# A decoder trunk on one core: the second layer's Gram masks, a pair's norm and T's diagonal blocks, each issued at another place

## The chip, the cores and the metric

The kernel runs on one core of a Trainium2 chip. Five engines take instructions from queues of their own, in order: TensorE (PE, matmuls and transposes; its weight loads are listed apart as PEld), VectorE (DVE), ScalarE (ACT), GpSimd (POOL) and SyncE (SP, which here only issues DMAs). An instruction starts when its engine is free and the semaphores it waits for are set. Matmul results land in PSUM, everything else is kept in SBUF. The metric is the time of the whole program on the device in microseconds (us); a change of 0.2% is 4.4 us here.

## What is computed

Two residual layers over 512 tokens of width 2048. Layer 0 is gated differential attention, layer 1 gated RWKV-7 time mixing. The change touches layer 1 alone. Cut to that layer:

```python
hn = rms_norm(x, norm_w[1])
p = hn @ w_in;  p = p + (token_shift(p) - p) * mu        # r, k, v, g, and two low-rank inputs
r, k, v, g, dw, da = split(p)
decay = exp(-exp(w_log(dw)));  a = sigmoid(a0 + da @ iclr_up)
kk = normalise(k * k_k);  k = k * (1 + (a - 1) * k_a)    # kk: per head of 64 channels
for t in range(512):                                     # per head, state S is 64 x 64
    S = S * decay_t + (S @ -kk_t) outer (kk_t * a_t) + v_t outer k_t
    y_t = S @ r_t
y = (y - mean) * rsqrt(var + eps) * gn_w + gn_b          # over a head's 64 channels
y = y + sum(r * k * r_k) * v
x = x + (y * silu(g)) @ w_out
```

All matrices are float32; products of large matrices are made from split operands (high and low part), three matmuls for each.

## The kernel before

**Pairs and periods.** Layer 1 handles the 32 heads as 16 pairs of heads (128 channels each), in `layer1`. For pair j it computes four projections, each of 16 row blocks times 3 matmuls of 128x512 (48 matmuls `pp` at L129): key (`proj(1, j)`), receptance (`proj(0, j)`, in `receptances`), value (`proj(2, j)`) and gate (`proj(3, ...)`, which lags three pairs behind). These matmuls fill PE; everything else of PE is put between them at counted places. One turn of the loop over j, from one value projection to the next, is called a period here.

**The scan.** The 512 steps of a head are cut into 8 chunks of 64 (C=64), and each chunk is handled by three dependent matmuls, all into one PSUM tile `sm`: a *state product* `sm<-VS,G` (L1341), copied out by ACT as `rhs` (L1344); a *solve product* `sm<-rhs,TT` (L1354), copied by ACT into `VS` (L1356); and an *update* `sm<-VS,BKT` (L1361), from which DVE makes the next chunk's state in `VS` (L1365, with `Sg` from POOL). The chunks are called steps 0 to 7. POOL saves each step's state first (`SA<-VS`, L1349, one copy for each head), and ACT may only overwrite `VS` with the solve product once POOL has done that. After step 7 the outputs `Y` are formed on PE from `VS` and `SA` (L1383, L1387) and centred by DVE (`centre`). Pair j-1's scan runs during pair j's period.

**The Gram matrices.** In pair j's value projection, behind its sixth row block, `gram` multiplies keys by queries: 16 matmuls into four PSUM tiles `gp`. ACT copies them to `G` in SBUF (L1140) and then copies the 32x32 diagonal blocks from `G` to `LP` (L1145). POOL zeroes the halves of `G` that lie beyond the diagonal with four `affine_select` (`mask_gram`, L1171 and L1173). For all pairs but the last that call hangs on the receptance projection of the next pair, but nothing ties the instructions to that matmul: the scheduler, which orders each engine's queue by dependencies and priority, puts them right behind the copies of `G`. The pair's scan reads `G` from the next period on.

**The triangular solve.** `t_solve` inverts the 32x32 blocks of all chunks at once on DVE: a transpose `LT<-LP` (L1202), then 31 steps of two small instructions (`tmpl` L1215, `Tm` L1218), two transposes to `T1` and `W`, and four POOL copies `TT<-W` (L1234). Its steps are let go by the count of projection matmuls that have been issued (`yield`), the first after 12. `t_first` and `t_second` complete `TT` on PE and ACT.

**A pair's norm.** `group_norm` takes ACT's square (`ysq`, L1408), DVE's sum, an inverse root of 11 small DVE instructions (`rs_i`, `rs_t`, L63 to L70) and the scaling of `yc` (L1414).

**Weights.** Each quarter of a 2048-row block of weights is split by ACT (`wh`, L115) and DVE (`wl`, L116) into tiles that are reused as PE finishes with them; these two instructions stand at many places between the others on both engines.

**Order.** Priorities (`high_priority` with AHEAD 2000, SOLVE 4000, SCAN 5000) and `issue_after` decide where the scheduler places an instruction. `behind` adds a dependency without a semaphore: it orders the schedule, but the engine does not wait for it.

Of the kernel before, what the change touches and what calls it, by code (L numbers as in the profile page):

```python
# [13 lines left out]
F32 = mybir.dt.float32  # L14
# [4 lines left out]
ALU = mybir.AluOpType  # L19
# [4 lines left out]
P = 128  # L24
# [14 lines left out]
AHEAD, SCAN, SOLVE = 2000, 5000, 4000  # L39
# [1086 lines left out]
def gram(g, j, p):  # L1126

    nc, w, BK = g.nc, g.work, p.BK
    p.G = w.tile([P, NC_, 2, 2, C], F32, name="G1", tag="G1", bufs=2)
    halves = []  # L1130
    for c0, tag in ((0, "pb"), (4, "pc")):
        gp = [g.ps.tile([P, 512], F32, name="gp", tag=tag, bufs=2) for _ in range(2)]
        halves.append((c0, gp))
        for i in range(4):
            for h, r_ in ((0, slice(0, C)), (1, slice(C, P))):
                m = nc.tensor.matmul(gp[h][:, i * P : (i + 1) * P], BK[r_, c0 + i, :, :], p.AR[r_, c0 + i, :, :],
                                     start=True, stop=True)
    for c0, gp in halves:
        for h in range(2):
            nc.scalar.copy(p.G[:, c0 : c0 + 4, :, h, :], gp[h][:].rearrange("p (u x t) -> p u x t", u=4, x=2))  # L1140
    p.LP = w.tile([P, NC_, HALF], F32, name="LP", tag="tmpl", bufs=1)
    for h in range(2):
        for half in range(2):
            q = slice(h * C + half * HALF, h * C + half * HALF + HALF)
            nc.scalar.copy(p.LP[q], p.G[q, :, 0, h, half * HALF : (half + 1) * HALF])  # L1145


def norms(g, j, p, m):
# [15 lines left out]
    nc.gpsimd.dma_start(out=p.n2[:], in_=nd.rearrange("h b r c t -> (h b r c) t"))  # L1164


def mask_gram(g, p, h):

    nc = g.nc
    for r_ in [slice(h * C, h * C + C)]:  # L1170
        nc.gpsimd.affine_select(out=p.G[r_, :, 0, 1 - h, :], in_=p.G[r_, :, 0, 1 - h, :], compare_op=ALU.is_ge,  # L1171
                                fill=0.0, base=-1, pattern=[[0, NC_], [1, C]], channel_multiplier=-1)
        nc.gpsimd.affine_select(out=p.G[r_, :, 1], in_=p.G[r_, :, 1], compare_op=ALU.is_ge, fill=0.0, base=0,  # L1173
                                pattern=[[0, NC_], [0, 2], [1, C]], channel_multiplier=-1)


def turn_keys(g, p, c0):
# [7 lines left out]
    nc.scalar.copy(p.BKT[:, c0 : c0 + 4], ps[:].rearrange("p (c k) -> p c k", c=4))  # L1185


def behind(g, ins):

    if g.at:  # L1190
        g.tc.add_manual_dep(ins.ins, g.at.ins.name, mybir.DependencyInfo(mybir.DependencyClass.NoSync,
                            mybir.DependencyReason.DATA), reason="pace")


def t_solve(g, j, p):


    nc, w = g.nc, g.work
    NQ = HALF // NG
    yield 12  # L1200
    LT = w.tile([P, HALF, HALF], F32, name="LT", tag="LT", bufs=1)
    lt = nc.vector.transpose(LT[:].rearrange("p (r c) t -> p t r c", r=NG),  # L1202
                        p.LP[:].rearrange("p c t -> p t c")[:, :, None, :].to_broadcast([P, HALF, NG, NC_]))
    Tm = w.tile([P, NQ, HALF], F32, name="Tm", tag="Tm", bufs=1)
    tmp = w.tile([P, NQ * HALF], F32, name="tmpl", tag="tmpl", bufs=1)
    nc.gpsimd.tensor_copy(Tm[:], g.unit[:])
    n2 = p.n2
    behind(g, lt)
    with g.tc.issue_after(lt.ins):
        nc.vector.tensor_scalar(n2[:], n2[:], 1e-24, None, ALU.max)  # L1210
        nc.vector.reciprocal(n2[:], n2[:])
    for i in range(HALF - 1):
        n, s = HALF - 1 - i, i // NG + 1
        tt = tmp[:, : n * s].rearrange("p (a b) -> p a b", a=s)
        st = nc.vector.scalar_tensor_tensor(tt, LT[:, i : i + 1, i + 1 :].to_broadcast([P, s, n]), n2[:, i : i + 1],  # L1215
                                       Tm[:, 0:s, i : i + 1].to_broadcast([P, s, n]), ALU.mult, ALU.mult)
        behind(g, st)
        nc.vector.tensor_add(Tm[:, 0:s, i + 1 :], Tm[:, 0:s, i + 1 :], tt)  # L1218
        yield 3 + i % 2
    nc.vector.tensor_mul(Tm[:], Tm[:], n2[:, None, :].to_broadcast([P, NQ, HALF]))  # L1220
    p.T1 = w.tile([P, NC_, HALF], F32, name="T1", tag="T1", bufs=1)
    yield 9
    tt = nc.vector.transpose(p.T1[:].rearrange("p c (q r) -> p q r c", r=NG),
                        Tm[:].rearrange("p q (r c) -> p q r c", r=NG))
    p.W = w.tile([P, NC_, HALF], F32, name="W", tag="Tm", bufs=1)
    behind(g, tt)
    yield 4
    tt = nc.vector.transpose(p.W[:], p.T1[:])
    behind(g, tt)
    for h in range(2):  # L1230
        for half in range(2):
            o = half * HALF
            q = slice(h * C + o, h * C + o + HALF)
            nc.gpsimd.tensor_copy(g.TT[j % 2][q, :, h, o : o + HALF], p.W[q])  # L1234
# [168 lines left out]
def group_norm(g, j, p):  # L1403
    p.chain.finish(g)
    nc, w, yc = g.nc, g.work, p.yc
    NG = 2 * NT
    sq = w.tile([P, NG, C], F32, name="ysq", tag="thg", bufs=1)
    nc.scalar.activation(sq[:], yc[:], AF.Square)  # L1408
    var = g.small.tile([P, NG], F32, name="var", tag="var")
    nc.vector.reduce_sum(var[:], sq[:], AX.X)  # L1410
    nc.vector.tensor_scalar(var[:], var[:], 1.0 / C, GN_EPS, ALU.mult, ALU.add)
    rs = g.small.tile([P, NG], F32, name="rsg", tag="rsg")
    rsqrt(g, rs[:], var[:], NG, "r8")
    nc.vector.tensor_mul(yc[:], yc[:], rs[:, :, None].to_broadcast([P, NG, C]))  # L1414
# [11 lines left out]
def layer1(g, aps):  # L1426
    nc, tc = g.nc, g.tc
    with ExitStack() as cx:
# [18 lines left out]
        def receptances(j):  # L1447
            def piece(f, i, p):
                def follow(m):
                    with tc.high_priority(offset=SCAN), tc.issue_after(m.ins):  # L1450
                        f(g, i, p)
                return follow

            behind = [(39, lambda m: norms(g, j, pairs[j], m))]
            if j:
                behind += [(6, lambda m: [mask_gram(g, pairs[j - 1], h) for h in range(2)]),
                           (12, piece(t_first, j - 1, pairs[j - 1])), (33, piece(t_second, j - 1, pairs[j - 1]))]
            return shift_mix(g, proj(0, j, behind=behind), P, *mus(g, 0, j), "r", 1)

# [2 lines left out]
        for j in range(D // P):  # L1462
# [29 lines left out]
            if j + 1 < D // P:  # L1492
                r = receptances(j + 1)
                if j:
                    group_norm(g, j - 1, pairs[j - 1])
        chain(g, j, p, 66, 5, 6, whole=True)
        gated(g, j - 2, pairs[j - 2], gate(g, j - 2, proj(3, j - 2)))
        gps = proj(3, j - 1)
# [118 lines left out]
```

## Time and profile before

| What | Value |
|---|---|
| median of 3 runs | 2188.4 us (2187.57 to 2192.0) |
| the profiled execution's own time | 2190.08 us |
| its span, first to last instruction | 2188.4 us |
| PE busy | 2138.8 us (98%) |
| DVE busy | 1555.2 us (71%) |
| ACT busy | 1118.5 us (51%) |
| POOL busy | 328.2 us (15%) |
| mean granted clock of PE | 0.996 |
| layer 1's periods | from about 1040 us to about 1960 us, some 62 us each |

Busy shares are of the span. PE's matmuls are pipelined, so that one of 128x512 is listed with about 0.4 us though the next starts 0.23 us after it. In a timeline row the columns are start, duration, engine, line, operation, out<-in, count, and in brackets the idle time of the engine just before and what ended it. A row of several instructions (x4) gives the time from the first's start to the last's end. "Granted clock" is the share of TensorE's full clock.

### The profile page before, as it was taken

The page shows a single profiled execution, that of the slowest core. Times are in us where ns is not written, and L with a number is a line of the kernel's source. Part 1 is how long each engine was busy: PE and PEld are TensorE (multiplying, and loading weights), DVE is VectorE, ACT ScalarE, POOL GpSimd, SP SyncE. Part 2 cuts the span into 40 slices and gives each one's busy share as a digit, 9 for nine tenths or more (in the row PEclk, how much of TensorE's full clock was granted, in tenths as well). Part 3 has the DMA queues.
Part 4 walks back from the last instruction along what each step waited for, and adds up shares of the span by engine and source line. Part 5 has one row for each costly group of instructions (what it writes and reads, how often), then busy time and mean ns, then how long its engine had stood idle before and what let it go on. Part 6 is the DMA issues. An engine that isn't in the chain of part 4 may idle for free.

```text
span 2188.4 us, 34852 instructions
## 1 busy us (share of the span) xinstructions
PE 2138.8 (98%) x12260; PEld 1755.7 (80%) x12260; DVE 1555.2 (71%) x4137; ACT 1118.5 (51%) x2523; POOL 328.2 (15%) x614
## 2 busy tenths in 40 slices
PE   9999999999999999999999999999999999999999
PEld 8888888888888878878777877777778777777887
DVE  5665646465665667476788888888888898887645
ACT  6443434344443454345566656555666565565333
POOL 0000000000000000120232222232222222332001
PEclk9999999999999999999999999999999999999999
DMA  7322232222222356563222222222222222245566
GB/s 194 93 83 96 87 97 92 92 91 88 92 87 97 117 182 223 153 137 82 75 60 65 76 76 65 78 75 75 75 75 76 75 66 78 80 126 183 174 167 122
DMA packets 258623, 225.76 MB, mean 103 GB/s; under 512 B 12336, under 2 KB 220480, under 8 KB 258448
## 3 DMA queue, kind: packets, MB, share of 16 engines
q1 hardware_dynamic: 239504, 188.03, 29.2%
q0 software_dynamic: 10080, 19.50, 4.5%
q10 hardware_dynamic: 8864, 16.01, 2.0%
q8 instruction: 96, 1.57, 0.3%
q14 instruction: 79, 0.65, 0.1%
HBM read 207.50 MB, written 15.99 MB: 102 GB/s over the span
## 4 chain that ended last, share of the span: by engine, by line
PE 83%; DVE 11%; ACT 2%; issue 2%; DMA 1%; POOL 0%; DVEq 0%; ACTq 0%; POOLq 0%
PE pp L129 65%; PE pt L129 5%; DVE wl L116 2%; DVE LT L1202 2%; PE sm L1341 1%; PE o L129 1%; PE sc L129 1%; DVE rs_t L68 1%; PE lora L129 1%; PE sm L1354 1%; PE sm L1361 1%; PE Y L1383 1%; DMA yr<-yd 1%; ACT wh L115 1%; PE pt L346 1%
## 5 line engine op out<-in xcount | busy, mean ns | idle before, releaser
L116 DVE TENSOR_TENSOR wl<-wraw,wh 128x512 fp32r<-128x512 f32 (+1 forms) x636 | 441.9, 697 | 399.0 <-ACT wh L115 386.3
L115 ACT CAST wh<-wraw 128x512 fp32r<-128x512 f32 (+1 forms) x636 | 393.5, 620 | 518.6 <-PE pp L129 413.9
L129 PE MATMUL pp<-wh,hH 128*128 128x512 f32 x1268 | 500.2, 394 | 0.8 <-DVE prmin_rw_mu_dram L234 0.7
L129 PE MATMUL pp<-wh,hL 128*128 128x512 f32 x1268 | 497.5, 393 | 0.0
L129 PE MATMUL pp<-wl,hH 128*128 128x512 f32 x1268 | 497.0, 392 | 0.0
L129 PE MATMUL pp<-hH,wh 128*128 128x512 f32 x1024 | 420.1, 410 | 0.0
L129 PE MATMUL pp<-hL,wh 128*128 128x512 f32 x1024 | 415.9, 406 | 0.0
L129 PE MATMUL pp<-hH,wl 128*128 128x512 f32 x1024 | 415.5, 406 | 0.0
L129 PEld LDWEIGHTS pp<-wh,hH 128*128 128x128 f32 x1268 | 238.3, 188 | 49.0 <-issue 1.3
L129 PEld LDWEIGHTS pp<-wh,hL 128*128 128x128 f32 x1268 | 238.2, 188 | 48.6 <-DVE hL L908 0.2
L129 PEld LDWEIGHTS pp<-wl,hH 128*128 128x128 f32 x1268 | 238.3, 188 | 46.9
L129 PEld LDWEIGHTS pp<-hH,wh 128*128 128x128 f32 x1024 | 194.9, 190 | 38.8 <-issue 2.1
L129 PEld LDWEIGHTS pp<-hH,wl 128*128 128x128 f32 x1024 | 194.8, 190 | 33.7
L129 PEld LDWEIGHTS pp<-hL,wh 128*128 128x128 f32 x1024 | 194.8, 190 | 32.3
L1349 POOL COPY SA<-VS 64x64 f32<-64x64 f32 x224 | 68.9, 307 | 510.5 <-DVE VS L1365 451.4
L1215 DVE SCALAR_TENSOR_TENSOR tmpl<-LT,n,Tm 128x60 f32<-128x60 f32 (+24 forms) x496 | 135.0, 272 | 13.3
L500 POOL DMA_DIRECT2D frow<-yd x12 | 8.9, 744 | 804.1 <-DVE rs_t L67 675.7
L1218 DVE TENSOR_TENSOR Tm<-Tm,tmpl 128x60 f32<-128x60 f32 (+24 forms) x496 | 104.2, 210 | 12.8
L1344 ACT COPY rhs<-sm 64x64 f32<-64x64 f32 x256 | 53.1, 207 | 85.5 <-PE sm L1341 83.5
L1341 PEld LDWEIGHTS sm<-VS,G 128*128 128x128 f32 x256 | 45.9, 188 | 50.4 <-issue 34.4
L1356 ACT COPY VS<-sm 64x64 f32<-64x64 f32 x256 | 53.1, 207 | 59.5 <-PE sm L1354 52.9
L1341 PE MATMUL sm<-VS,G 128*128 128x128 f32 x256 | 51.2, 282 | 31.7 <-DVE VS L1365 30.2
(339 smaller groups left out, 3285.4 us busy)
## 6 DMA issues: line engine op xcount, KB each, us to landing
wraw<-in_rw_w_in_dram SPq DMA_DIRECT2D x128, 512.0 KB, 4.0
wraw<-in_da_w_in_dram SPq DMA_DIRECT2D x254, 256.0 KB, 3.0
wraw<-in_da_w_out_dram SPq DMA_DIRECT2D x26, 512.0 KB, 4.5
wraw<-in_rw_w_out_dram SPq DMA_DIRECT2D x26, 512.0 KB, 4.2
yr<-yd SPq DMA_DIRECT2D x28, 256.0 KB, 3.9
frow<-yd POOLq DMA_DIRECT2D x12, 512.0 KB, 6.1
xq<-in_x_dram SPq DMA_DIRECT2D x16, 256.0 KB, 5.5
xd<-xq ACTq DMA_DIRECT2D x16, 256.0 KB, 3.8
```

The source lines that it names most:

```text
L68: nc.vector.scalar_tensor_tensor(t[:], t[:], -0.5, v, ALU.mult, ALU.mult)
L115: nc.scalar.copy(hi[:], raw[:, k : k + n])
L116: nc.vector.tensor_sub(lo[:], raw[:, k : k + n], hi[:].bitcast(F32))
L129: m = nc.tensor.matmul(out, a, b, start=s, stop=e, skip_group_check=skip)
L346: nc.tensor.transpose(pt[:, c * P : (c + 1) * P], t1s[t][:, c * P : (c + 1) * P], g.ident[:])
L1202: lt = nc.vector.transpose(LT[:].rearrange("p (r c) t -> p t r c", r=NG), p.LP[:].rearrange("p c t -> p t c")[:, :, None, :].to_broadcast( ...
L1215: st = nc.vector.scalar_tensor_tensor(tt, LT[:, i : i + 1, i + 1 :].to_broadcast([P, s, n]), n2[:, i : i + 1], Tm[:, 0:s, i : i + 1].to_br ...
L1218: nc.vector.tensor_add(Tm[:, 0:s, i + 1 :], Tm[:, 0:s, i + 1 :], tt)
L1341: nc.tensor.matmul(sm[:, 0:P], both(p.G[:, c, 0]), both(VS[:, c]), start=True, stop=True)
L1344: rc = nc.scalar.copy(rhs[r_, :], sm[r_, h * C : h * C + C])
L1349: nc.gpsimd.tensor_copy(p.SA[r_, c - 1, :], VS[r_, c, h, :])
L1356: nc.scalar.copy(VS[r_, c, h, :], sm[r_, P : P + C])
```

## The change

Three parts, all in layer 1.

1. `mask_gram` gets the sixth matmul of the next pair's receptance projection and ties its instructions to it with `behind`, an ordering without a semaphore.
2. `group_norm` of a pair, in the loop, is issued with priority AHEAD.
3. `LP` is copied from the PSUM tiles `gp` and not from `G`: eight copies of 32x128 with priority AHEAD, in place of four of 32x256; the copies of `G` keep their form. `t_solve` starts after 9 matmuls in place of 12.

```diff
+    p.LP = w.tile([P, NC_, HALF], F32, name="LP", tag="tmpl", bufs=1)
+    with g.tc.high_priority(offset=AHEAD):
+        for c0, gp in halves:
+            for h in range(2):
+                for half in range(2):
+                    q, o = h * C + half * HALF, half * HALF
+                    nc.scalar.copy(p.LP[q : q + HALF, c0 : c0 + 4],
+                                   gp[h][q : q + HALF].rearrange("p (u x) -> p u x", u=4)[:, :, o : o + HALF])
     for c0, gp in halves:
         for h in range(2):
             nc.scalar.copy(p.G[:, c0 : c0 + 4, :, h, :], gp[h][:].rearrange("p (u x t) -> p u x t", u=4, x=2))
-    p.LP = w.tile([P, NC_, HALF], F32, name="LP", tag="tmpl", bufs=1)
-    for h in range(2):
-        for half in range(2):
-            q = slice(h * C + half * HALF, h * C + half * HALF + HALF)
-            nc.scalar.copy(p.LP[q], p.G[q, :, 0, h, half * HALF : (half + 1) * HALF])
...
-def mask_gram(g, p, h):
+def mask_gram(g, p, h, m=None):
...
-        nc.gpsimd.affine_select(out=p.G[r_, :, 0, 1 - h, :], in_=p.G[r_, :, 0, 1 - h, :], compare_op=ALU.is_ge,
+        a = nc.gpsimd.affine_select(out=p.G[r_, :, 0, 1 - h, :], in_=p.G[r_, :, 0, 1 - h, :], compare_op=ALU.is_ge,
...
-        nc.gpsimd.affine_select(out=p.G[r_, :, 1], in_=p.G[r_, :, 1], compare_op=ALU.is_ge, fill=0.0, base=0,
+        b = nc.gpsimd.affine_select(out=p.G[r_, :, 1], in_=p.G[r_, :, 1], compare_op=ALU.is_ge, fill=0.0, base=0,
...
+        behind(g, a, m)
+        behind(g, b, m)
...
-    yield 12
+    yield 9
...
-                behind += [(6, lambda m: [mask_gram(g, pairs[j - 1], h) for h in range(2)]),
+                behind += [(6, lambda m: [mask_gram(g, pairs[j - 1], h, m) for h in range(2)]),
...
-                    group_norm(g, j - 1, pairs[j - 1])
+                    with tc.high_priority(offset=AHEAD):
+                        group_norm(g, j - 1, pairs[j - 1])
```

What it moves is seen in the engines' queues. The rows below are from one period in the middle of layer 1; the periods from pair 3 to pair 14 read alike. Line numbers from L1144 on are 3 to 7 higher in the changed kernel.

POOL, the end of one scan and the start of the next, before (`SA` and `Sg` serve a scan step, `TT` the solve, the `AFFINE_SELECT` are the masks; the first `SA` here is of step 7, the second of step 1 of the next scan):

```order
L1349 COPY SA<-VS 64x64 x2
L1234 COPY TT_10025<-W 32x8x32 x4
L1338 MEMSET VS 64x64 x2
L1206 CAST Tm<-unit 128x256
L1161 DMA nd<-ssl 2x4x256 x2
L1164 DMA n_16966<-nd 128x32
L1349 COPY SA<-VS 64x64 x2
L1352 TENSOR_SCALAR Sg<-SA,gam 128x64
L1171 AFFINE_SELECT G_17045<-G_17045 64x8x64 x2
L1173 AFFINE_SELECT G_17045<-G_17045 64x8x128 x2
```

The same stretch of POOL in the changed kernel, where the first row belongs to step 6:

```order
L1358 TENSOR_SCALAR Sg<-SA,gam 128x64
L1174 AFFINE_SELECT G_16364<-G_16364 64x8x64
L1240 COPY TT_10025<-W 32x8x32 x4
L1355 COPY SA<-VS 64x64
L1176 AFFINE_SELECT G_16364<-G_16364 64x8x128
L1355 COPY SA<-VS 64x64
L1174 AFFINE_SELECT G_16364<-G_16364 64x8x64
L1176 AFFINE_SELECT G_16364<-G_16364 64x8x128
L1344 MEMSET VS 64x64 x2
L1212 CAST Tm<-unit 128x256
L1164 DMA nd<-ssl 2x4x256 x2
L1167 DMA n_17006<-nd 128x32
```

The four masks have left the place behind the Gram matmuls and step 1, and stand at the end of the scan before theirs: one ahead of the `TT` copies, one between the two `SA` copies of step 7, two behind; the `TT` copies now stand ahead of both `SA` copies of step 7.

DVE, from the end of a pair's norm to the state of scan step 2 (`yc` is the norm's last instruction), before:

```order
L1414 TENSOR_TENSOR yc<-yc,rsg 128x512
L116 TENSOR_TENSOR wl<-wraw,wh 128x512
L1202 STREAM_TRANSPOSE LT<-LP 128x32x32
L1210 TENSOR_SCALAR n_16966<-n_16966 128x32
L1211 RECIPROCAL n_16966<-n_16966 128x32
L1215 SCALAR_TENSOR_TENSOR tmpl<-LT,n_16966,Tm 128x31
L1218 TENSOR_TENSOR Tm<-Tm,tmpl 128x31
L116 TENSOR_TENSOR wl<-wraw,wh 128x512
L1365 SCALAR_TENSOR_TENSOR VS<-sm,gam,Sg 64x64 x2
```

and in the changed kernel:

```order
L1420 TENSOR_TENSOR yc<-yc,rsg 128x512
L1208 STREAM_TRANSPOSE LT<-LP 128x32x32
L1216 TENSOR_SCALAR n_17006<-n_17006 128x32
L116 TENSOR_TENSOR wl<-wraw,wh 128x512
L1217 RECIPROCAL n_17006<-n_17006 128x32
L1221 SCALAR_TENSOR_TENSOR tmpl<-LT,n_17006,Tm 128x31
L1224 TENSOR_TENSOR Tm<-Tm,tmpl 128x31
L1221 SCALAR_TENSOR_TENSOR tmpl<-LT,n_17006,Tm 128x30
L1224 TENSOR_TENSOR Tm<-Tm,tmpl 128x30
L116 TENSOR_TENSOR wl<-wraw,wh 128x512
L1371 SCALAR_TENSOR_TENSOR VS<-sm,gam,Sg 64x64 x2
```

The transpose stands ahead of the first `wl`, and one more solve step stands ahead of the state `VS`; the norm keeps its place between step 1's state and the transpose.

ACT, from the norm's square to the update of scan step 1 (`rhs` is that step's state product), before:

```order
L1408 ACTIVATE ysq<-yc 128x512
L1140 COPY G_17045<-gp 128x8x64 x4
L1145 COPY LP<-G_17045 32x256 x2
L115 CAST wh<-wraw 128x512
L1344 COPY rhs<-sm 64x64 x2
L1145 COPY LP<-G_17045 32x256 x2
L1356 COPY VS<-sm 64x64 x2
```

and in the changed kernel:

```order
L1414 ACTIVATE ysq<-yc 128x512
L1144 COPY LP<-gp 32x128 x4
L1148 COPY G_17085<-gp 128x8x64 x2
L1144 COPY LP<-gp 32x128 x4
L1148 COPY G_17085<-gp 128x8x64 x2
L115 CAST wh<-wraw 128x512
L1350 COPY rhs<-sm 64x64 x2
L1362 COPY VS<-sm 64x64 x2
```

All copies to `LP` now stand ahead of `rhs`, where two of four stood before. PE's queue has the same order in both kernels from pair 3 on.

7 lines of the change are left out of this document (4 added, 3 removed).

## The prediction

> **What bounds the kernel now.** I read the page's first part, then who waited for whom, then the chain that ended last, and last one period's timeline on each engine.
>
> ```profile
> span 2188.4 us, 34852 instructions
> PE 2138.8 (98%) x12260; PEld 1755.7 (80%) x12260; DVE 1555.2 (71%) x4137; ACT 1118.5 (51%) x2523; POOL 328.2 (15%) x614
> PE sm L1341 <- DVE VS L1365: 28.0, 12, 2.6
> ```
>
> PE is the bound: it is idle for 2188.4 - 2138.8 = 49.6 us only. The change adds and removes no matmul, so all that it can move is this idle time and PE's clock. The third row is from the waits of 1200 to 1900 us: in twelve periods PE stands still once, for 28.0 / 12 = 2.33 us, until DVE has made the state of a scan step (step 2). That is over half of all idle time. One of the twelve, on PE, DVE, POOL and ACT in turn:
>
> ```profile
> 1446.29 0.33 PE L1354 MATMUL sm<-rhs,TT 128*128 128x64 f32 x2
> 1453.08 0.46 PE L1341 MATMUL sm<-VS,G 128*128 128x128 f32 x2 [2.30 <-DVE VS L1365]
> ...
> 1441.65 0.69 DVE L1410 TENSOR_REDUCE var<-ysq 128x8 f32<-128x512 f32 x1
> 1443.62 0.17 DVE L67 TENSOR_TENSOR rs_t<-rs_i 128x8 f32<-128x8 f32 x1
> 1443.82 0.52 DVE L68 SCALAR_TENSOR_TENSOR rs_t<-rs_t,var 128x8 f32<-128x8 f32 x1
> 1445.11 1.08 DVE L68 SCALAR_TENSOR_TENSOR rs_t<-rs_t,var 128x8 f32<-128x8 f32 x1
> 1446.43 1.53 DVE L1414 TENSOR_TENSOR yc<-yc,rsg 128x512 f32<-128x512 f32 x1
> 1447.89 0.68 DVE L116 TENSOR_TENSOR wl<-wraw,wh 128x512 fp32r<-128x512 f32 x1
> 1448.49 2.19 DVE L1202 STREAM_TRANSPOSE LT<-LP 128x1024 f32<-128x1024 f32 x1
> 1450.59 0.13 DVE L1210 TENSOR_SCALAR n<-n 128x32 f32<-128x32 f32 x1
> 1451.62 0.69 DVE L116 TENSOR_TENSOR wl<-wraw,wh 128x512 fp32r<-128x512 f32 x1
> 1452.34 0.60 DVE L1365 SCALAR_TENSOR_TENSOR VS<-sm,gam,Sg 64x64 f32<-64x64 f32 x2
> 1452.97 0.31 DVE L1215 SCALAR_TENSOR_TENSOR tmpl<-LT,n,Tm 128x30 f32<-128x30 f32 x1
> 1453.54 0.25 DVE L1215 SCALAR_TENSOR_TENSOR tmpl<-LT,n,Tm 128x29 f32<-128x29 f32 x1
> ...
> 1443.63 1.43 POOL L1171 TENSOR_SCALAR_AFFINE_SELECT G<-G 64x512 f32<-64x512 f32 x2 [1.10 <-ACT G L1140]
> 1445.03 2.40 POOL L1173 TENSOR_SCALAR_AFFINE_SELECT G<-G 64x1024 f32<-64x1024 f32 x2
> ...
> 1441.93 2.05 ACT L1140 COPY G<-gp 128x512 f32<-128x512 f32 x4 [1.09 <-PE gp L1136]
> 1443.85 0.82 ACT L1145 COPY LP<-G 32x256 f32<-32x256 f32 x2
> 1445.22 0.42 ACT L1344 COPY rhs<-sm 64x64 f32<-64x64 f32 x2
> 1447.41 0.62 ACT L115 CAST wh<-wraw 128x512 fp32r<-128x512 f32 x1 [0.26 <-PE pp L129]
> ```
>
> No DVE row from the norm's sum at 1441.65 to step 2's state at 1452.34 shows idle time ahead of it: the stall is the length of this queue. Two things in it are long: the transpose `LT`, and the norm while POOL's masks run. Norm instructions that otherwise need 0.17 us take 0.52 and 1.08 and end where a mask ends (POOL's second pair of masks starts at 1445.03 and takes 1.20 each); the scaling of `yc` takes 1.53 us.
>
> **The masks leave the norm (part 1).** With 0.20 us from one norm instruction to the next (1443.62 to 1443.82), five of them lead from 1443.62 to `rsg` at 1444.64, and `yc` comes at 1444.85 in place of 1446.43. For `yc` I take the multiply of its size, 0.68:
>
> ```profile
> 1417.45 0.68 DVE L1092 TENSOR_TENSOR f<-f,mixk 128x512 f32<-128x512 f32 x1
> L1344 ACT COPY rhs<-sm 64x64 f32<-64x64 f32 x179 | 37.1, 207 | 63.5 <-PE sm L1341 62.2
> L1252 ACT COPY X<-px 32x256 f32<-32x256 f32 x22 | 8.1, 367 | 0.4
> L1140 ACT COPY G<-gp 128x512 f32<-128x512 f32 x44 | 22.6, 600 | 12.0 <-PE gp L1136 12.0
> ```
>
> So the norm ends at about 1445.5, not at 1447.96.
>
> **The transpose earlier (part 3).** `LT` follows `yc` directly, at 1445.5 if `LP` is there by then (below: 1445.04). It holds DVE 2.10 us (1448.49 to 1450.59), so `n` comes at 1447.6. From `n` to the `wl` ahead of the state took 1.03 us with one solve step in it; now another `wl` (0.60, 1447.89 to 1448.49) and another solve step (0.57, 1452.97 to 1453.54) lie there too: 2.20, so `wl` at 1449.8 and the state, 0.72 behind it as before, at 1450.52. The state's start led PE's restart by 1453.08 - 1452.34 = 0.74; PE could go on at 1451.26. PE comes to this matmul at 1453.08 - 2.30 = 1450.78. DVE alone would leave a stall of 0.48 us.
>
> **What ACT pays.** All eight small copies now stand ahead of `rhs`, where two of 0.41 us did. None of this form (32x128 from PSUM) is in the trace. The nearest rows are 207 ns for 64 elements and 367 ns for 256; on a line between them 128 elements cost 0.26 us, which I take, with the two rows as the ends. `rhs` moves by 8 x 0.26 - 0.82 = 1.26 us. It ended at 1445.64, PE used it at 1446.29, and at least 0.14 lies between (as from the state's end at 1452.94 to 1453.08), so 0.51 was spare. PE will wait 0.75 us at step 1's solve product; by the ends 0.33 and 1.61. `LP` is complete after eight copies and two of `G` (2.05 / 4 each): 1441.93 + 2.08 + 1.03 = 1445.04. The later end of the `G` copies, 2.1 us, costs nothing: their readers, masks and scan, come in the next period.
> [...] The row of `rhs`, two copies in 0.42 us, shows no overlap, so the sum stays with 0.26.
>
> The two waits do not add. PE that waits 0.75 us at step 1 comes to step 2 at 1451.53, when the state is there. A period loses the larger of the two: 0.75 in place of 2.33. Gain 1.58 x 12 = **19.0 us**; by the ends, (2.33 - 1.61) x 12 = 8.6 to (2.33 - 0.48) x 12 = 22.2.
>
> **The norm's priority (part 2).** DVE's and ACT's queues hold the norm where it was. Nothing, from pair 3 on; ahead of that see pairs 0 to 2.
>
> **The clock.** Some stalls cost more than their length:
>
> ```profile
> 1328.00:1333.00 5.00, 5.00 (x18) 4.02 (x17) 4.65 (x16) 2.02 (x6) 0.29 (x1) 0.66 0.19 42
> 1390.00:1395.00 5.00, 4.03 (x20) 3.42 (x21) 4.56 (x16) 1.52 (x5) 0.95 (x3) 1.00 0.01 2
> 1891.00:1896.00 5.00, 5.00 (x18) 4.05 (x18) 4.66 (x16) 1.83 (x6) 0.48 (x1) 0.66 0.15 28
> 1323.04 2.11 DVE LT L1202
> 1386.47 2.10 DVE LT L1202
> 1448.57 2.11 DVE LT L1202
> ```
>
> The first three rows are stretches right behind a stall; the third number from the end is the granted clock. It is 0.66 behind four of the twelve stalls (the first and the last are shown) and 1.00 behind the others. The chain's `LT` rows give the periods: 63.43 us with such a dip, 62.10 without; 1.33 each, 4 x 1.33 = **5.3 us**. A stall of 0.75 us is a third of those that only sometimes bring a dip, so I take the dips as gone; the other end is that they stay, and cost this 5.3.
>
> **The masks' new place.** POOL now copies `TT`, then `SA`, makes a mask, and copies the other `SA`; ACT may write step 7's solve product only behind its `SA`, and `Y` reads that.
>
> ```profile
> 1390.23 0.28 DVE VS L1365
> 1422.28 0.72 DVE L949 SCALAR_TENSOR_TENSOR mixv<-pp,prmin_rw_mu_dram,mixv 128x511 f32<-128x511 f32 x1
> 1423.54 0.45 DVE L1228 STREAM_TRANSPOSE W<-T 128x256 f32<-128x256 f32 x1
> 1423.64 0.24 POOL L1349 COPY SA<-VS 64x64 f32<-64x64 f32 x1 [0.16 <-DVE VS L1365]
> 1424.05 3.73 POOL L1234 COPY TT<-W 32x256 f32<-32x256 f32 x4 [0.17 <-DVE W L1228]
> 1426.62 0.44 ACT L1356 COPY VS<-sm 64x64 f32<-64x64 f32 x2 [0.19 <-POOL TT L1234]
> 1427.84 1.20 PE L1383 MATMUL Y<-VS,G 128*64 128x64 f32 x32
> ```
>
> `W` started 33.3 us behind step 2's state. Now `mixv` and step 7's state (1422.28 to 1423.54, 1.26) come behind it and one solve step (0.57) has gone ahead: 31.5, plus up to 0.7 while the first mask holds DVE up (1.43 / 2). The state leads PE's step 2 by 1.01 now (1450.52 to 1451.53). Counted from PE's step 2, 1390.23 + 0.74 = 1390.97 in this period, `TT` starts at 31.0 to 31.7 and ends 3.73 later; then `SA` 0.25, mask 1.20, `SA` 0.25, at 37.1 at most, and ACT's copy ends by 37.3. PE starts `Y` at 1427.84 - 1390.97 = 36.9 and needs step 7 last, at some 37.8. It fits by 0.5 us, so I take nothing. The two masks behind that may hold `wl` and the centring up by as much as they take, 0.7 + 1.2, before the next norm; whether that matters is in the first rival.
>
> **Pairs 0 to 2** have other orders and smaller waits; PE's queue moves there too. I put +0.5 us on them, 1.5 either way.
>
> **The sum** goes against the profiled execution: 2190.08 - 19.0 - 5.3 + 0.5 = 2166.3. The median of the runs is 1.7 below that execution, so **2164.6 us**.
>
> **Rivals.**
> - *The masks hold step 7 up.* If `W` comes no earlier than before (33.1 for `TT`), the last copy ends at 33.1 + 3.73 + 1.7 + 0.2 = 38.7, 0.9 us late in twelve periods: 10.8 less gain, 2175.4. That masks slow DVE speaks for it, the new place of `W` against. [...]
> - *ACT becomes the bound: slower.* If a small copy costs as much as the large one, 600 ns, `rhs` is late by 8 x 0.60 - 0.82 - 0.51 = 3.5 us, the dips stay, and the time is 2188.4 + 12 x (3.5 - 2.33) = 2202. It decides from (2.33 + 0.82 + 0.51) / 8 = 0.46 us a copy on. The rows of 207 and 367 ns speak against.
> - *Nothing happens.* The masks' tie sets no semaphore, and step 2's state still stands behind a `wl`, which needs its `wh`. Were PE's release of that `wh` the true end of the wait, the stall would stay: 2187. Against it: `wh` was released at 1447.41, so with PE's new wait it is written by 1448.8, and DVE comes to its `wl` at 1449.8.
>
> **How the numbers follow.** The forecast, 2160 to 2172 by its ends and those of pairs 0 to 2: 0.62. Masks hold step 7 up, 2172 to 2180: 0.20. Nothing happens: 0.06. Slower: 0.08. Below 2160, where pairs 0 to 2 gain too: 0.04. The range of 2159 to 2180 leaves out under 0.2. About 0.2%, 4.4 us, is what a measurement can tell from no change: faster 0.87, same 0.05, slower 0.08.
>
> **What would show it.** Right: the norm's `rs_t` rows near 0.17 us and `yc` near 0.7; the idle time ahead of `sm<-VS,G` gone or under 0.3 us; a new wait of some 0.75 us of `sm<-rhs,TT` for ACT's `rhs`, twelve times; clock 1.00 throughout 1200 to 1900; periods of 60.5 us. Wrong: copies to `LP` of over 0.4 us; idle time ahead of `Y`; a scan step from 3 to 7 that waits for DVE.

## The result, and the profile after

The changed kernel takes 2168.09 us (median of 4 runs, 2167.57 to 2170.35) against 2188.87 us for the kernel before (4 runs, 2187.57 to 2192.0): a ratio of 0.9905, with a 95% interval of 0.9888 to 0.9922. That is 20.8 us less; 23.8 were forecast (2188.4 to 2164.6), and the range held the time. The profiled execution took 2167.93 us, 22.15 less than the one before; all of the accounts below go against it.

The page's first part, of the kernel after:

```profile
span 2166.2 us, 34954 instructions
PE 2132.2 (98%) x12260; PEld 1755.7 (81%) x12260; DVE 1544.3 (71%) x4137; ACT 1124.0 (52%) x2587; POOL 334.1 (15%) x614
```

PE is idle for 34.0 us in place of 49.6. Who waited for whom on PE from 1200 to 1900 us (total, times, longest):

```profile
PE sm L1360 <- ACT rhs L1350: 6.6, 12, 0.6
```

The stall at step 2 (28.0 us in twelve periods) is not in the list any more, and a wait for ACT's `rhs` has come, at step 1. One period's timeline, PE, DVE, POOL and ACT in turn, at the places that the prediction showed of before:

```profile
1442.85 0.43 PE L1360 MATMUL sm<-rhs,TT 128*128 128x64 f32 x2 [0.55 <-ACT rhs L1350]
1447.29 0.38 PE L1347 MATMUL sm<-VS,G 128*128 128x128 f32 x2
...
1437.49 0.69 DVE L1416 TENSOR_REDUCE var<-ysq 128x8 f32<-128x512 f32 x1
...
1440.26 0.17 DVE L68 SCALAR_TENSOR_TENSOR rs_t<-rs_t,var 128x8 f32<-128x8 f32 x1
1440.66 0.69 DVE L1420 TENSOR_TENSOR yc<-yc,rsg 128x512 f32<-128x512 f32 x1
1441.27 2.15 DVE L1208 STREAM_TRANSPOSE LT<-LP 128x1024 f32<-128x1024 f32 x1
1446.06 0.60 DVE L1371 SCALAR_TENSOR_TENSOR VS<-sm,gam,Sg 64x64 f32<-64x64 f32 x2
...
1413.28 1.20 POOL L1174 TENSOR_SCALAR_AFFINE_SELECT G<-G 64x512 f32<-64x512 f32 x1
...
1437.77 1.06 ACT L1144 COPY LP<-gp 32x128 f32<-32x128 f32 x4 [1.09 <-PE gp L1136]
1439.80 1.06 ACT L1144 COPY LP<-gp 32x128 f32<-32x128 f32 x4
...
1442.37 0.43 ACT L1350 COPY rhs<-sm 64x64 f32<-64x64 f32 x2
```

From the norm's sum to step 2's state DVE now takes 1446.06 - 1437.49 = 8.57 us, where it took 1452.34 - 1441.65 = 10.69. The norm's instructions take 0.17 us each, `yc` 0.69, and no mask runs beside them: in the period whose `gp` begins at 1376.43 the first mask stands at 1413.28, beside the solve's tail, where it stood 2.9 us behind `gp`, beside the norm. PE reaches step 2 at 1447.29, 1.23 us after the state's first instruction has started, and doesn't wait.

The clock in the first of the stretches that the prediction showed, kernel after (the third number from the end):

```profile
1328.00:1333.00 5.00, 5.00 (x28) 4.22 (x27) 4.72 (x15) 2.81 (x7) 0.23 (x1) 1.00 0.37 102
```

It reads 1.00 where 0.66 stood. Where the time went can be told in four pieces, by the start of the Gram product `gp` on PE, which begins each pair. For all kernels of this study, from their traces (us; the last column is the median of the runs):

| kernel | pair 0 to pair 3 | PE idle in it | half-clock windows in it | twelve periods, 3 to 15 | pair 15 to the end | median of the runs |
|---|---|---|---|---|---|---|
| before | 150.58 | 7.84 | 1 | 751.22 | 246.32 | 2188.87 |
| after | 155.68 | 12.72 | 2 | 721.98 | 248.26 | 2168.09 |
| masks' tie alone | 149.07 | 8.19 | 0 | 734.20 | 246.32 | 2171.81 |
| copies from PSUM and earlier solve alone | 153.72 | 9.61 | 3 | 730.09 | 248.19 | 2172.51 |
| after, solve after 12 | 152.42 | 12.04 | 0 | 743.60 | 247.43 | 2186.26 |
| after, two G copies late | 153.35 | 11.35 | 1 | 722.79 | 248.19 | 2166.73 |
| after, old ends | 149.25 | 8.27 | 0 | 721.98 | 246.36 | 2159.69 |
| G late, whole solve later, masks at 24 | 155.02 | 10.25 | 4 | 764.90 | 247.46 | 2211.17 |
| after, masks at 24 | 160.96 | 14.77 | 4 | 721.93 | 248.28 | 2172.51 |
| old ends, rhs and state both early | 149.23 | 8.16 | 0 | 714.91 | 246.31 | 2152.44 |
| after, old LP copies at the ends | 152.82 | 11.68 | 0 | 721.99 | 246.91 | 2164.63 (one run) |
| after, solve after 12 at the ends | 155.15 | 11.90 | 2 | 721.93 | 247.44 | 2165.3 (one run) |

The change gains 29.24 us in the twelve periods, loses 5.10 in the three pairs ahead of them and 1.94 behind: 29.24 - 5.10 - 1.94 = 22.20, and pair 0 starts 0.05 later.

A half-clock window is one of the clock's dips, 3.41 us at a granted clock of 0.50. These are the two that the changed kernel has in pairs 0 to 2; the kernel before has one there, at 1055.84 us:

```profile
1056.36:1059.77 3.41, 3.41 (x10) 2.64 (x9) 2.50 (x9) 1.99 (x5) 0.00 (x0) 0.50 0.30 87
1148.52:1151.93 3.41, 3.41 (x13) 2.92 (x12) 2.55 (x6) 1.03 (x4) 1.08 (x3) 0.50 0.00 0
```

In the steady periods of the kernel before, a dip cost 1.33 us (63.43 us against 62.10). So a difference of one or two microseconds in pairs 0 to 2 can be the clock's, and the two columns are to be read beside it.

### The profile page after: what moved, and what is told of

The parts are those of the page before. It is cut to its first block, busy times and chain, and to the rows that moved or that the text cites. A ratio compares the mean times of both kernels' runs of the same rounds, so it can differ in the third digit from the quotient of the medians.

```text
span 2166.2 us, 34954 instructions
## 1 busy us (share of the span) xinstructions
PE 2132.2 (98%) x12260; PEld 1755.7 (81%) x12260; DVE 1544.3 (71%) x4137; ACT 1124.0 (52%) x2587; POOL 334.1 (15%) x614
## 4 chain that ended last, share of the span: by engine, by line
PE 89%; DVE 5%; ACT 4%; issue 1%; DMA 1%; POOL 0%; DVEq 0%; ACTq 0%; POOLq 0%
PE pp L129 69%; PE pt L129 5%; ACT G L1148 1%; ACT LP L1144 1%; PE o L129 1%; PE sc L129 1%; PE sm L1360 1%; PE sm L1367 1%; PE sm L1347 1%; PE lora L129 1%; DVE wl L116 1%; PE gp L1136 1%; PE Y L1389 1%; DMA yr<-yd 1%; PE pt L346 1%
## 5 line engine op out<-in xcount | busy, mean ns | idle before, releaser
L116 DVE TENSOR_TENSOR wl<-wraw,wh 128x512 fp32r<-128x512 f32 (+1 forms) x636 | 446.8, 705 | 388.3 <-ACT wh L115 379.3
L1355 POOL COPY SA<-VS 64x64 f32<-64x64 f32 x224 | 78.6, 351 | 470.5 <-DVE VS L1371 411.2
L1224 DVE TENSOR_TENSOR Tm<-Tm,tmpl 128x60 f32<-128x60 f32 (+24 forms) x496 | 112.0, 226 | 13.0
L1360 PEld LDWEIGHTS sm<-rhs,TT 128*128 128x128 f32 x256 | 46.1, 188 | 29.9 <-ACT rhs L1350 18.4
L1371 DVE SCALAR_TENSOR_TENSOR VS<-sm,gam,Sg 64x64 f32<-64x64 f32 x192 | 54.1, 282 | 20.0 <-PE sm L1367 15.4
```

The costliest lines, as they stand in the source:

```text
L116: nc.vector.tensor_sub(lo[:], raw[:, k : k + n], hi[:].bitcast(F32))
L1355: nc.gpsimd.tensor_copy(p.SA[r_, c - 1, :], VS[r_, c, h, :])
L1360: nc.tensor.matmul(sm[:, P : P + C], both(g.TT[j % 2][:, c]), rhs[:], start=True, stop=True)
L1371: g.state = nc.vector.scalar_tensor_tensor(VS[r_, c + 1, h, :], s_, p.gam[r_, c : c + 1], Sg[r_, :], ALU.mult, ALU.add)
```

## The experiments

The theory after the result: the steady gain is the prediction's mechanism, and the seven microseconds lost at both ends come from pieces meant for the steady pairs. The rivals: one part does it all; the new wait for `rhs` is what is left to win; the masks' tie causes the losses.

Part 2 (the norm's priority) has no run of its own. With it undone, the order of the instructions is word for word that of the changed kernel on PE, DVE, ACT and POOL, in the whole program. It moves nothing here.

**The masks' tie alone (part 1).** Before, with this:

```
-                behind += [(6, lambda m: [mask_gram(g, pairs[j - 1], h) for h in range(2)]),
+                behind += [(6, lambda m: [mask_gram(g, pairs[j - 1], h, m) for h in range(2)]),
...
+        behind(g, a, m)
+        behind(g, b, m)
```

> Part 1 alone: the masks are tied as in the change, the rest is as before. Theory A (the stall at scan step 2 is the length of DVE's queue, and the masks lengthen it by holding norm instructions up): the norm's rs_t rows fall to 0.17 us and yc to 0.7; the transpose LT then waits for the old copies of LP, at the same place in ACT's queue as before (complete at 1446.5 in the period of before), so it starts 1.9 us earlier than before; the stall of 2.33 us falls to about 0.4; no wait for rhs at step 1, the four dips of the clock gone: 2190 - 12 x 1.9 - 5.3 = 2162 us. In this kernel's POOL queue two masks stand ahead of step 7's SA copies; if they hold DVE there, steps 6 or 7 wait up to 0.7 us in twelve periods, 2170. Rival B (the gain came from the earlier transpose and LP, and the norm is slow for another reason): stall stays at 2.3 us, 2188. Rival C (masks cost at the new place what they cost at the old): stall at step 2 gone but steps 6, 7 or Y wait about 2 us, 2185 to 2190.

Measured: 2171.81 us, ratio 0.9925 (0.9913 to 0.9938). Its waits on PE from 1200 to 1900 us:

```profile
PE sm L1344 <- DVE VS L1368: 10.4, 23, 0.7
PE px L1252 <- DVE T L1226: 1.5, 9, 0.2
```

and step 7's timeline in one period, on PE, DVE and POOL:

```profile
1417.36 0.46 PE L1344 MATMUL sm<-VS,G 128*128 128x128 f32 x2 [0.54 <-DVE VS L1368]
...
1410.41 0.64 DVE L1221 TENSOR_TENSOR Tm<-Tm,tmpl 128x24 f32<-128x24 f32 x1
1411.58 1.12 DVE L1218 SCALAR_TENSOR_TENSOR tmpl<-LT,n,Tm 128x16 f32<-128x16 f32 x1
1414.23 0.17 DVE L1221 TENSOR_TENSOR Tm<-Tm,tmpl 128x8 f32<-128x8 f32 x1
1416.63 0.58 DVE L1368 SCALAR_TENSOR_TENSOR VS<-sm,gam,Sg 64x64 f32<-64x64 f32 x2
...
1409.82 1.21 POOL L1171 TENSOR_SCALAR_AFFINE_SELECT G<-G 64x512 f32<-64x512 f32 x1
1410.99 1.68 POOL L1173 TENSOR_SCALAR_AFFINE_SELECT G<-G 64x1024 f32<-64x1024 f32 x1
```

23 waits in twelve periods are two in each: 0.34 us at step 2, where 2.33 stood, and a new one of 0.54 at step 7. Leaving the norm is worth 2 us a period at step 2. But POOL meets two masks ahead of step 7's copies here, and they hold solve steps on DVE as they held the norm (0.64 and 1.12 us, where the same two take 0.18 and 0.23 in the kernel before), so that step 7's state is late. That is the case for which the expectation had 2170. In the changed kernel one mask lies there. The two long rows end within 0.05 us of a mask's end, at 1411.05 and 1412.70 against 1411.03 and 1412.67: the slowing went with the masks to their new place. What causes it the rows do not show. Pairs 0 to 2 lose nothing. They take 1.5 us less, though PE is idle for no less (8.19 us against 7.84): the dip of the kernel before is missing. The masks' tie is not what costs the ends.

**The copies from PSUM and the earlier solve alone (part 3).** The changed kernel without the two `behind(g, a, m)` and `behind(g, b, m)`, and without the norm's priority, which moves nothing. (The run above is without it too.)

> Part 3 alone: LP from PSUM and the solve after 9 matmuls; masks as before, right behind the copies of G. Theory A: those copies now end 2 us later, so the masks start when the norm is over and run beside the transpose and the instructions behind it; a wait of 0.55 us for rhs at step 1, and n, wl and the first solve steps held up by up to one mask (1.2 us) each, so that step 2 still waits 0.5 to 1.5 us: 2173 to 2186 us. Rival B (the earlier transpose brings the gain): as the changed kernel, 2168.

Measured: 2172.51 us, ratio 0.9924 (0.991 to 0.9937):

```profile
PE sm L1358 <- ACT rhs L1348: 6.0, 11, 0.5
PE sm L1345 <- DVE VS L1369: 5.5, 12, 0.5
```

Each part alone brings most of the gain (17.1 and 16.4 us of 20.8), since each alone shortens the queue ahead of the state to within half a microsecond of what PE leaves it. They don't add. The two waits are those of theory A, and the time is just under its range. The cost at the ends is here: 3.1 us more than before in pairs 0 to 2 (1.8 of it idle time, with two more half-clock windows), 1.9 in the last.

**The solve after 12 steps again.** Masks' tie and copies from PSUM stay:

```
-    yield 9
+    yield 12
```

> The changed kernel with the solve let go after 12 matmuls again: in DVE's queue wl stands ahead of the transpose, and waits for a wh that stands behind all copies of LP and G on ACT. Theory A: the transpose starts about 1.8 us later than in the changed kernel, step 2 waits about 0.9 us in addition to 0.55 at step 1, in twelve periods: 2168 + 11 = 2179 us, without dips of the clock or with one or two. Rival B (masks alone made the gain): 2168, same as the changed kernel.

Measured: 2186.26 us, ratio 0.999 (0.9981 to 0.9999).

```profile
PE sm L1347 <- DVE VS L1371: 13.2, 23, 0.6
PE sm L1360 <- ACT rhs L1350: 6.4, 12, 0.5
```

Three waits in a period: `rhs` 0.53, step 2 0.60, and step 7 0.55 again. Neither theory had that third wait. The one number is worth 18.2 us, not only for the transpose: with the solve later, two masks stand ahead of step 7's copies on POOL, as in the run with the tie alone, and hold DVE there.

**Two of the four G copies behind step 1's `rhs`.** In the changed kernel:

```
-    for c0, gp in halves:
...
+    whole(*halves[0])
+    if 0 < j < D // P - 1:
+        g.soon.append(lambda: whole(*halves[1]))
```

> The changed kernel with the last two copies of G put behind step 1's rhs (the two ahead of it and all of LP stay). Theory A (the 0.55 us at step 1 is ACT's queue: rhs comes behind 12 copies): the wait for rhs goes; DVE's queue has wl ahead of the transpose here and the state of step 2 comes 0.25 us later, so 0.2 to 0.3 us of stall are left at step 2: 12 x 0.25 = 3 us less, and pairs 1 and 2, which wait 1.5 and 3.1 us for rhs in the changed kernel, give 2 us more: 2163 us. Rival (DVE's queue would hold step 2 as long anyway): 2168, with the wait moved to step 2 in full.

Measured: 2166.73 us, ratio 0.9897 (0.9883 to 0.9911).

```profile
PE sm L1353 <- DVE VS L1377: 8.0, 12, 0.7
```

The wait for `rhs` is gone and step 2 waits again, 0.66 us: the period is 60.23 against 60.16. `wh` now comes earlier too, and its `wl` goes ahead of the transpose and waits there. ACT's `rhs` and DVE's state are two bounds side by side, much as the rival said. The 2.3 us in pairs 0 to 2 are the gain, 1.4 of them idle time, and one dip fewer.

**The old way at both ends.** The changed kernel, with LP from `G` and the solve after 12 in pairs 0 to 2 and 15 alone:

```
-    with g.tc.high_priority(offset=AHEAD):
+    if LAG <= j < D // P - 1:
...
-    yield 9
+    yield 9 if LAG <= j < D // P - 1 else 12
```

> The changed kernel, with the way of before put back in pairs 0 to 2 and in the last pair for two of its parts: LP is copied from G behind the G copies, and the solve waits twelve steps instead of nine; the masks stay tied, and pairs 3 to 14 are as changed. Theory A: the 5.15 us that pairs 0 to 2 lost, and the 1.9 us that the last pair lost, come from the eight small copies ahead of rhs (and from the earlier solve) where ACT has more to do; the kernel should begin pair 3 no later than 1.0 us behind the kernel before (5.15 in the changed kernel), keep the period of 60.15 us, and take 2161 to 2163. Rival B: the loss comes from the masks' tie or from the mere shift of PE's queue; then it stays, and the time is 2167 to 2169.

Measured: 2159.69 us, ratio 0.9872 (0.9855 to 0.9888). Theory A holds, though the time is 1.3 us under its range: 6.4 us come back in pairs 0 to 2, 1.9 in the last, and the twelve periods are the same to a hundredth. Of the 6.4, 4.45 are idle time of PE; both dips are gone too. PE's waits from 1035 to 1200 us, of the changed kernel, the two largest:

```profile
PE sm L1360 <- ACT rhs L1350: 4.9, 3, 3.1
PE pt L1297 <- DVE Tm L1224: 3.0, 1, 3.0
```

and the same two of this one:

```profile
PE pt L1307 <- DVE Tm L1234: 2.0, 1, 2.0
...
PE sm L1370 <- ACT rhs L1360: 1.1, 3, 0.6
```

Step 1's `rhs` kept PE waiting for 1.5 us in pair 1 and 3.1 in pair 2; here 0.3 us at most before pair 3 (the 0.6 is already pair 3's own). In pair 1 ACT works through the copies without a pause until `rhs`. In pair 2 the copies are half of it only. ACT stands still ahead of the norm's square `ysq` (the changed kernel, then the kernel before):

```profile
1142.85 0.63 ACT L1414 ACTIVATE ysq<-yc 128x512 f32<-128x512 f32 x1 [2.72 <-DMA nd<-ssl]
1147.10 0.42 ACT L1350 COPY rhs<-sm 64x64 f32<-64x64 f32 x2
...
1137.95 0.62 ACT L1408 ACTIVATE ysq<-yc 128x512 f32<-128x512 f32 x1
1141.53 0.45 ACT L1344 COPY rhs<-sm 64x64 f32<-64x64 f32 x2
```

In the kernel's code `ysq` is written into the one buffer that `ssl` (the keys' sums of squares, on their way to `n`) had before, so it waits until two DMAs have read `ssl`. POOL issues them, in the changed kernel here:

```profile
1136.94 1.18 POOL L1164 DMA_DIRECT2D nd<-ssl x2 [0.21 <-issue]
```

In every kernel whose solve starts after 9 matmuls in this pair, and isn't held up further, both stand behind the four copies `TT<-W` on POOL; in the kernel before the first is issued at 1130.34, ahead of these copies. Counted from the start of pair 2's `gp`, `rhs` is copied at 3.11 us in the kernel before, at 4.77 with the copies from PSUM and the solve after 12, at 4.84 with the old copies and the solve after 9 (a run below), and at 6.53 with both: each is worth 1.7 us there.

In the last pair the changed kernel waits 1.4 us for ACT's `VS` and 1.1 for DVE's state (1900 to 1960 us); here the whole is 0.5.

**Both bounds relieved by moving the whole solve and the masks.** In the changed kernel with late G copies:

```
         nc.vector.reciprocal(n2[:], n2[:])
+    yield 14
...
-                behind += [(6, lambda m: [mask_gram(g, pairs[j - 1], h, m) for h in range(2)]),
+                behind += [(24, lambda m: [mask_gram(g, pairs[j - 1], h, m) for h in range(2)]),
```

> The changed kernel with the last two G copies behind step 1's rhs, as in the run before with the late copies (period 60.21 us, step 2 waited 0.66 us for DVE's state), and in addition the solve's first two steps behind step 2's state in DVE's queue (about 0.5 us each, some 1.0 us off the queue ahead of the state) and the masks tied to the 24th receptance matmul in place of the 6th. TT's four copies now stand behind three of the masks on POOL. Theory A: the steady period has two bounds side by side, ACT's rhs (0.55 us) and DVE's state (0.66 us behind it); with both relieved step 1 and step 2 wait for nothing, the restart cost of some 0.2 us goes too, the period is 59.3 to 59.6 us and the time 2154 to 2160. Rival B: a third wait is just behind the two (step 7 or Y, since T's solve and TT come later); then the period stays at 59.9 to 60.3 and the time is 2163 to 2169, with idle time at step 7 or at the product ahead of it.

Measured: 2211.17 us, ratio 1.0104 (1.0089 to 1.0119): slower than both theories, and than the kernel before.

PE's wait from 1200 to 1900 us, and one period's timeline:

```profile
PE px L1262 <- DVE gam L1108: 25.4, 11, 2.3
```

```profile
1503.60 0.69 PE L1262 MATMUL px<-T,G 32*32 32x32 f32 x32 [2.30 <-DVE gam L1108]
...
1498.96 1.09 POOL L1180 TENSOR_SCALAR_AFFINE_SELECT G<-G 64x512 f32<-64x512 f32 x1
...
1499.45 0.62 DVE L1231 TENSOR_TENSOR Tm<-Tm,tmpl 128x8 f32<-128x8 f32 x1
1500.59 1.37 DVE L1233 TENSOR_TENSOR Tm<-Tm,n 128x256 f32<-128x256 f32 x1
1502.94 0.60 DVE L1236 STREAM_TRANSPOSE T<-Tm 128x256 f32<-128x256 f32 x1
```

The waits at steps 1 and 2 are gone but for 1.2 us in the first period, as A said. But the solve is let go 14 matmuls later, and its tail lies beside the masks: the last step's sum takes 0.62 us and the scaling by `n` 1.37 (0.16 and 0.41 in the changed kernel), and `px` needs T. (The wait is put down to `gam`, the small instruction of DVE that ends together with the transpose `T`, at 1503.54.) Eleven half-clock windows stand in the twelve periods besides, where the changed kernel has none. Rival B had the place nearly right and the price far too low. Delay and collision were moved together, so how much each costs isn't told apart by this run; the next two help.

**The masks at the 24th matmul, alone.** The changed kernel with 24 for 6 in that line.

> The changed kernel with one number changed: the masks are tied to the 24th receptance matmul, not the 6th, which puts them behind TT and both SA copies of step 7 on POOL. Theory A (the prediction's: the masks' new place costs nothing, it fits by some 0.3 to 0.5 us ahead of Y): the time is that of the changed kernel, 2166.5 to 2169.5, with the period of 60.15 us. Rival B: four masks take 5.3 us and now reach into the norm; the norm's instructions on DVE stretch again, step 2 waits 0.6 us or more, and the time is 2173 to 2182.

Measured: 2172.51 us, ratio 0.9923 (0.9909 to 0.9938). The time fits neither expectation; the traces tell why. The twelve periods are unchanged, 721.93 us: the masks behind step 7's copies and behind TT bring nothing, so their place at the 6th costs the steady pairs nothing. The 5.3 us are all lost in pairs 0 to 2, where `px` waits for T up to 2.9 us and the clock dips for two windows more (idle time is 2.1 of the 5.3):

```profile
PE px L1255 <- DVE T L1229: 5.5, 3, 2.9
```

**Both bounds relieved, the solve's end kept.** The kernel with the old ends, and in pairs 3 to 14:

```
+        for it in g4[:2]:
+            whole(*it)
+        g.soon.append(lambda: [whole(*it) for it in g4[2:]])
...
+    mid = LAG <= j < D // P - 1
+    if mid:
+        yield 14
...
-        yield 3 + i % 2
+        yield 3 + i % 2 - (mid and 2 <= i < 16)
```

> The kernel of the last run but two (old LP copies and solve after twelve steps in pairs 0 to 2 and 15), and in pairs 3 to 14 the two bounds relieved together with the end of the solve left where it was: the last two G copies stand behind step 1's rhs on ACT; the first two solve steps (some 1.0 us on DVE) stand behind step 2's state, and 14 of the later solve steps are spaced one pace shorter, so that T, W and TT keep their places; the masks stay at the 6th matmul. Theory A: with rhs 1.0 us and the state some 0.5 us earlier (1.0 us of solve steps less, 0.5 us for the wl ahead of the transpose more), the wait of 0.55 us at step 1 and that of 0.66 us at step 2 are both gone; the period falls from 60.15 to 59.3 to 59.6 us, and the time from 2159.7 to 2150 to 2154. Rival B: a third wait stands behind these two whatever the solve's end does (steps 3 to 7 or the product with T, G); then the period stays at 59.8 to 60.2 and the time at 2156 to 2161.

Measured: 2152.44 us, ratio 0.9835 (0.9821 to 0.9848). Theory A holds, in the time and in the period. It is the fastest kernel of the study, 36 us under the one before. Its stretch of 1200 to 1900 us (PE's busy time is the second number):

```profile
1200.00:1900.00 700.00, 699.98 (x4947) 573.82 (x4946) 614.65 (x1641) 443.21 (x1100) 210.34 (x402) 1.00 0.30 80
```

and step 4 on PE in one period:

```profile
1511.50 0.46 PE L1363 MATMUL sm<-VS,G 128*128 128x128 f32 x2
```

PE has 0.02 us of idle time in 700; the changed kernel had 6.62. The period is 59.58 us on average, 59.49 in most and up to 59.79 in some: of the 0.82 us won at step 1 a part is lost at later steps, as in this row, in waits too short to show as idle (below). Against the run with the whole solve later, the first solve steps are moved by the same 14; with the end kept and the masks left at the 6th matmul the twelve periods take 714.91 us in place of 764.90, and no half-clock window is left in them.

**Which old piece mends the ends.** The old LP copies in pairs 0 to 2 and 15, the solve after 9 everywhere:

> The changed kernel with the old LP copies (from G, behind it) in pairs 0 to 2 and 15 alone; the solve waits nine steps everywhere. The two old pieces together brought pairs 0 to 2 from 5.15 us behind the kernel before to 1.50 us ahead of it, and the last pair's 1.9 us back. Theory A: ACT's queue is the cause (the waits for rhs of 1.5 us in pair 1 and 3.1 us in pair 2); then this piece alone brings pair 3's start to between 1.5 us ahead and 1.5 us behind, and the wait ahead of the last pair's steps is gone; 2160 to 2163. Rival B: the earlier solve on DVE is the cause; then pair 3 still starts 3.5 to 5 us behind, 2164 to 2168.

and the counterpart, the solve after 12 in those pairs, the copies from PSUM everywhere:

> The counterpart: the changed kernel with the solve after twelve steps in pairs 0 to 2 and 15 alone, and the small copies straight from PSUM in all pairs. Theory A (ACT's copies are the cause): pair 3 starts 3.5 to 5 us behind the kernel before, only the wait behind Tm in pair 0 shrinks from 3.0 to 2.1 us; 2164 to 2168. Rival B (the earlier solve is the cause): pair 3 starts within 1.5 us of the kernel before; 2160 to 2163.

Their largest waits on PE from 1035 to 1200 us, the first kernel and then the second:

```profile
PE sm L1357 <- DVE VS L1381: 3.9, 3, 1.4
PE pt L1307 <- DVE Tm L1234: 1.9, 1, 1.9
PE sm L1370 <- ACT rhs L1360: 1.9, 3, 1.5
```

```profile
PE pt L1297 <- DVE Tm L1224: 3.6, 1, 3.6
PE sm L1360 <- ACT rhs L1350: 3.6, 3, 1.7
```

Neither expectation holds. From pair 0 to pair 3 the old copies bring 2.86 us, the old place of the solve 0.53, both together 6.43; in the last pair 1.35, 0.82 and 1.90. Part of the first is the clock: with the old copies no dip is left, with the old place of the solve alone both are. Of PE's idle time the old copies bring 1.0 us, the old place of the solve 0.8, both together 4.5. With the old copies alone `rhs` still waits 1.5 us in pair 2, behind a `ysq` that again stands still for 2.72 us, and the solve runs ahead of the state on DVE (3.9 us, 1.4 at the longest). With the solve alone `rhs` still waits behind the copies, 1.6 us in pair 1 and 1.7 in pair 2. So the loss belongs to both pieces, by paths of their own: the copies by ACT's queue, the earlier solve by DVE's queue and by way of POOL's DMAs. Why their idle times don't add up over the three pairs is open. The wait behind `Tm` in pair 0 goes with the copies (1.9 with the old, 3.6 with the new), not with the solve as I had expected. These two are single runs; the traces carry the reading.

## Why the prediction was right, and where it was off

*What bounds it.* Right: one wait a period, DVE's queue. The shortening of that queue by either part alone took 1.9 to 2.0 us off it.

*Part 1, the norm.* Right: `rs_t` rows of 0.17 and `yc` of 0.69 (0.17 and 0.68 were taken).

*Part 3, the state.* Right within 0.2 us: the state was to lead PE's step 2 by 1.01 us and leads it by 1.23.

*ACT's price.* Right: the profile has 257 ns for a copy to `LP` (260 were taken, between 207 and 367), and `rhs` moved by 1.32 us against the start of `gp` (1.26). The trace has 0.265 us from one copy to the next (four in 1.06), no less than a copy's own 0.257, so that here the copies from PSUM don't overlap.

*A period's gain.* The mechanism was right, its size too small: 1.58 us were taken. The eight periods without a dip gained 1.98 on average (2.13 the first, 1.95 to 1.97 the others), which is 23.7 in twelve in place of 19.0. The term was made of two unlike quantities, an idle time (2.33) and a delay (0.75). The view counts idle time from the end of the matmul before, but matmuls that follow one another start 0.23 us apart and last 0.39. Set start against start over one period, a wait with 2.30 of idle time had cost 2.53, the new one with 0.55 costs 0.82 (0.72 until the first of the two matmuls, close to the 0.75 forecast, and 0.10 until the second). The last 0.27 were at step 3, in a wait that shows no idle time at all:

```profile
1459.56 0.39 PE L129 MATMUL pp<-hH,wl 128*128 128x512 f32 x1
1459.98 0.46 PE L1341 MATMUL sm<-VS,G 128*128 128x128 f32 x2
```

This is the kernel before. `sm` starts 0.42 us behind its neighbour in place of 0.23, and the pair takes 0.46 in place of 0.38. DVE's queue was late there too. 2.53 + 0.27 - 0.82 = 1.98, where this period gained 1.95.

*The clock.* Right: no dip is left from 1200 to 1900 us, and the four periods that had one gained 13.43 us, 5.5 more than four without (5.3 were taken).

*Masks' new place, norm's priority.* Right: nothing, from pair 3 on, by the run with the masks at the 24th matmul and by the unchanged order.

*Pairs 0 to 2.* The step that failed. "Other orders and smaller waits" was priced at +0.5 (1.5 either way), and it was +5.10: PE's idle time there went from 7.84 to 12.72 us, and the clock dips twice in place of once. I hadn't followed the queues there. On ACT the eight copies stand ahead of `rhs`, as in the other pairs, and the wait for it is 1.5 us in pair 1. In pair 2 it is 3.1, half of it from the copies and half because `ysq` waits for DMAs that POOL issues behind the copies of `TT` once the solve is earlier. Putting the old copies and the old place of the solve back brought 6.4 us.

*The last pair.* No term stood for it; it cost 1.94, and the same two old pieces brought 1.90 back.

*The sum.* 4.9 us too little gain in the periods (the clock's share included) and 4.6 + 1.9 too little loss at the ends nearly cancel: 2167.93 against a sum of 2166.3. The closeness of the total is in part luck. "Masks hold step 7 up" was no empty rival: it happens, at 0.55 us a period, in both kernels in which the solve comes later (the masks' tie alone, and the solve after 12), by way of DVE. "ACT becomes the bound" is what happened in pair 1, and in part in pair 2, though not by the price that the rival named: a copy took 257 ns there as elsewhere.

## What to carry to other kernels

A step that is moved ahead for the steady loop is moved in the first and last turns too, where other work stands in the queues; price those turns from their own rows, or leave them as they were, which was worth 8.4 us here. When a wait goes, look at the engine next to it before moving more: ACT's `rhs` and DVE's state bounded the period within 0.1 us of each other, and relieving `rhs` alone gained nothing, both together 0.6 us a period. And keep the end of a moved chain of work where it was: the same first solve steps moved later gave a period of 63.7 us on average with the end moved too (and the masks with it; the two aren't told apart), and 59.6 with the end kept. Last, an instruction that is far from the change can share a buffer with one that the change delays, as `ysq` does with `ssl`: look at what a longer idle time is said to wait for before putting it down to the queue.

## What the runs showed of the hardware

In the traces of the two kernels the clock's dips stand on a grid. A dip lasts 3.41 us at a granted clock of 0.50. In the kernel before four come 187.73 us apart, 55 times 3.413, from 1328.91 us on; in the changed kernel the dips at 981.26, 1056.36 and 1148.52 us are 22 and 27 times 3.413 apart. The windows of this grid with a long stall in them can be compared. The first row here, of the kernel before, is followed by a dip, the second isn't; the third, of the run with the whole solve later, is followed by one:

```profile
1513.23:1516.64 3.41, 1.48 (x8) 1.30 (x9) 3.01 (x12) 1.25 (x4) 0.95 (x3) 1.00 0.26 77
1574.67:1578.08 3.41, 1.61 (x8) 0.99 (x6) 3.19 (x7) 1.03 (x2) 0.00 (x0) 1.00 0.58 154
...
1198.70:1202.11 3.41, 2.09 (x48) 1.50 (x44) 3.03 (x13) 3.27 (x11) 2.04 (x5) 1.00 0.00 0
```

The window ahead of a dip was not idle: PE was busy for 1.48 of 3.41 us in the first row. In the kernel before, from 50 to 2185 us, every window with up to 1.48 us of busy PE brought a dip and none with 1.61 or more did. So it mattered here how much of a stall lay within one window and how much beyond its edge: of the twelve stalls at step 2 (2.33 us on average, 2.6 the longest), four left PE 1.36, 1.48, 1.24 and 1.36 us in one window, and a dip followed; the other eight left it 1.61 or more. PE's busy time alone isn't the whole rule: in the third row 2.09 us brought a dip, and in the fastest kernel a window with 1.54 (1052.56 to 1055.97 us) brought none.

A wait of under some 0.16 us (0.39 - 0.23) leaves no idle time in the profile, since the matmul before it is still listed as running. It shows in the pair of small matmuls behind it, 0.46 us in place of 0.38.
